# The third q/k pair of the last two heads by seven block products, and rotated rows copied back by GpSimd

## The chip, the cores and the metric

The kernel runs on one core of a Trainium2 chip. The metric is the device time of one execution in microseconds (us); three executions of the kernel before took 808.54, 808.99 and 809.23 us, so its median is 808.99 us. Five engines work beside each other: TensorE (PE) multiplies matrices, VectorE (DVE) and ScalarE (ACT) work on elements, GpSimd (POOL) does a few small operations and issues some of the DMAs, SyncE (SP) issues the other DMAs. PE writes to PSUM, the others read PSUM or SBUF; GpSimd works on SBUF alone.

## The reference, cut to what matters

One layer of an encoder trunk on 512 positions of width 1024, all in float32. The normed input `n` is projected by one large weight; of that projection, 12 heads (3 groups of dilation 1, 4 and 16, with 4 heads each) get a query and a key of 128 features per position. The first 32 features of each are rotated by position, then come windowed scores, softmax, the sum over values, and a mixture of the three groups:

```
proj = jnp.einsum('bsd,de->bse', n, w_in[l])
z_gmlp, q, k, v, gates = jnp.split(proj, split_points, axis=-1)
q = partial_rope(q.reshape(B, S, n_heads, HEAD_DIM))
k = partial_rope(k.reshape(B, S, n_heads, HEAD_DIM))
...
o_g, lse_g = dilated_window_attention(q[:, :, sl], k[:, :, sl], v[:, :, sl], dilation, window // (2 * dilation))
```

`partial_rope` gives `x1 * cos - x2 * sin` and `x2 * cos + x1 * sin` in the 32 rotated features and leaves the other 96 as they are. A gated gMLP branch, a merge, an output projection and an MLP with 4096 hidden features follow.

## The kernel before, in words

**Products of float32 by three.** Every large product splits its two operands into a high and a low part (type fp32r): ACT copies the high part (lines 74 and 79), DVE subtracts it from the value to get the low part (lines 75 and 80). PE then multiplies high by high, high by low and low by high (`mm3`, lines 84 to 86, or line 343).

**Two ways to project a q/k pair.** A pair is the query and the key of one head index in one group; its weight is a tile `qkw` of 128 x 8 x 2 x 128 (512 KB for q, 512 KB for k, loaded by SP at line 66). The plain way (`feature_tile`) takes, for q and then for k, 8 blocks of the contraction by three matmuls of 512 columns: 48 matmuls of 512 columns for a pair, into one PSUM bank each, and ACT copies the result out at line 449, once for the 32 rotated rows (`st`) and once for all 128. The other way (`seven_qk`) cuts contraction, features and positions in halves and makes the 2 x 2 block product with seven products in place of eight. Its left operands are sums of weight blocks: `seven` (lines 329 to 334) makes the sums on DVE and splits them. Each of the seven products is 4 blocks by three matmuls of 256 columns, so a pair takes 84 matmuls of 256 columns, on three of the four PSUM banks named `acc`. Between the products ACT and DVE take intermediate results out (`p1`, `z5`, `u2`, `u3`, lines 399 to 414), and a later product into the same bank waits for them. The right operands `nmov` are made once, for all positions.

**The order.** `project_qk(h)` goes through the groups of head h. Groups 0 and 1 go the seven-product way; then come the rotation of both pairs (`rotate` over 4 tiles) and the scores of group 0 (`scores_a`). Then `attend(h - 1)`, the value sums of the head before, and the loads of the values for head h (`load_v`, two DMAs on GpSimd's queue at line 305). Group 2 goes the plain way, then its rotation (2 tiles) and `scores_b`. `rotate` gathers the 32 rows of each tile in `st`, shuffles and multiplies them on DVE (lines 419 to 422), and then copies 32 x 512 back to each tile, on ACT (line 424): 6 copies for a head, 24 in all. In `scores_a` the tiles are first split by ACT and DVE (`q0h`, `q0l`, `k0h`, `k0l`).

The framework's scheduler puts each engine's instructions into a fixed order when the kernel is built: each instruction may move up as soon as its inputs are there in the scheduler's own model of time, and program order decides between several. On the chip each engine then takes its instructions in that order. Buffers come from pools with a fixed number of slots; weights and the sums `s` share three slots of the tag `raw`. The stage with the heads lies at 81 to about 245 us of the profiled execution; the gMLP part, the gates and the MLP follow.

Of the kernel before, what the change touches and what calls it, by code (L numbers as in the profile page):

```python
# [12 lines left out]
AF = mybir.ActivationFunctionType  # L13
# [23 lines left out]
def block_kernel(ctx: ExitStack, tc: tile.TileContext, x, norm_mix_pre, w_in, b_gate, ln_v_gain, ln_v_bias,  # L37
                 w_spatial, b_spatial, w_branch_a, w_branch_b, w_out, norm_mix_post, norm_mlp_pre, w_up,
                 w_down, norm_mlp_post, ident_c, rope_c, mask_c, perm_c, out):
    nc = tc.nc  # L40
# [22 lines left out]
    def wload(shape, srcs, name):  # L63
        raw = wpool.tile([P] + shape, F32, name=name, tag="raw")
        for dst, src in srcs(raw):
            nc.sync.dma_start(dst, src)
        return raw

    def wsplit(raw, pl=None, bufs=None, tag="w", sub=None):
        pl = pl or wpool  # L70
        shape = list(raw.shape)
        hi = pl.tile(shape, F32R, name="hi", tag=tag + "hi", bufs=bufs)
        lo = pl.tile(shape, F32R, name="lo", tag=tag + "lo", bufs=bufs)
        nc.scalar.activation(hi, raw, AF.Copy)  # L74
        (sub or nc.vector).tensor_tensor(lo, raw, hi.bitcast(F32), op=ALU.subtract)  # L75
        return hi, lo
# [210 lines left out]
    def feature_tile(wh, wl, nk, mh, ml, tag="acc"):  # L287
        ps = psA.tile([P, S], F32, name="pf", tag=tag, bufs={"acc": 4, "S": 2, "T": 1, "y": 1}[tag])
        for k in range(nk):
            mm3(ps, (wh[:, k], wl[:, k]), (mh[:, k], ml[:, k]), k == 0, k == nk - 1)  # L290
        return ps

    def fcols(wap, c0, nk, n, raw=None):
        return wap[:, c0:c0 + n].rearrange("(k p) c -> p k c", p=P)
# [6 lines left out]
    def load_v(h):  # L301
        hs = slice(h * HD, (h + 1) * HD)
        v0, v12 = vpool.tile([P, 2, 4, HD], F32R, name="v0s"), vpool.tile([P, 2, 4, HD], F32, name="v12s")
        for src, dst in ((v0d, v0), (v12d, v12)):
            nc.gpsimd.dma_start(dst.rearrange("p a b c -> p (a b) c"), src[:, :, :, hs].rearrange("p a b c -> p (a b) c"))
        heads[h] = v0, v12
# [77 lines left out]
    def seven_qk(raw, g, c2, c1):  # L384

        w = seven(raw.rearrange("p k r c -> p k (r c)"), wsum, wsplit, split1)
        Y, Z, X = [psA.tile([P, 512], F32, name="pg", tag="acc", bufs=4)[:, A] for _ in range(3)]
        if g:
            view = lambda ps: ps.rearrange("p (l r) -> p r l", r=4)
            half = lambda d, i: d.rearrange("p (r h l) -> p h r l", r=4, h=2)[:, i]  # L390
            snap = lambda nm: qkpool.tile([P, 4, 64], F32, name=nm)
        else:
            view = lambda ps: ps
            half = lambda d, i: d[:, (A, B)[i]]
            snap = lambda nm: qkpool.tile([P, 4, 64], F32, name=nm).rearrange("p r l -> p (r l)")
        p1, z5, u2, u3 = snap("p1"), snap("z5"), snap("u2"), snap("u3")
        product(6, Y, w, nmov, True)
        product(1, X, w, nmov, True)
        taken = nc.scalar.activation(p1, view(X), AF.Copy)
        if pending:  # L400
            with tc.issue_after(taken.ins):
                pending.pop()()
        nc.vector.tensor_tensor(u2, view(Y), p1, op=ALU.add)
        product(5, Z, w, nmov, True)
        nc.scalar.activation(z5, view(Z), AF.Copy)
        product(2, X, w, nmov, False)
        nc.scalar.activation(half(c1, 0), view(X), AF.Copy)
        product(7, Y, w, nmov, False)
        nc.vector.scalar_tensor_tensor(u3, view(Y), -1.0, p1, op0=ALU.mult, op1=ALU.subtract)
        product(3, Z, w, nmov, False)  # L410
        nc.vector.tensor_tensor(half(c1, 1), view(Z), u2, op=ALU.add)
        nc.vector.tensor_tensor(half(c2, 1), u3, z5, op=ALU.subtract)
        product(4, Y, w, nmov, False)
        nc.vector.scalar_tensor_tensor(half(c2, 0), view(Y), -1.0, p1, op0=ALU.mult, op1=ALU.subtract)

    def rotate(st, tiles, r0):
        rows = slice(r0, r0 + 32 * len(tiles))
        sw = apool.tile([P, S], F32, name="sw")
        nc.vector.stream_shuffle(sw[rows], st[rows], [(i + 16) % 32 for i in range(32)])
        nc.vector.tensor_tensor(st[rows], st[rows], rope[rows, 0], op=ALU.mult)  # L420
        nc.vector.tensor_tensor(sw[rows], sw[rows], rope[rows, 1], op=ALU.mult)
        nc.vector.tensor_tensor(st[rows], st[rows], sw[rows], op=ALU.add)
        for i, d in enumerate(tiles):
            nc.scalar.activation(d[0:32], st[r0 + 32 * i:r0 + 32 * i + 32], AF.Copy)

    def project_qk(h):
        got, tiles, r0 = {}, [], 0
        load_v(h) if not h else None
        st = apool.tile([P, S], F32, name="st", bufs=2)
        for g in range(3):  # L430
            if g == 2:
                st, tiles, r0 = apool.tile([P, S], F32, name="st", bufs=2), [], 64
                if h:
                    attend(h - 1)
                    load_v(h)
            hd0 = (g * NH + h) * HD
            raw = wload([KD, 2, P], lambda r: [(r[:, :, 0], fcols(w_in, COL_Q + hd0, KD, P)), (r[:, :, 1], fcols(w_in, COL_K + hd0, KD, P))], "qkw")
            pair = [apool.tile([P, S], F32, name=f"{nm}{g}") for nm in "qk"]
            if g < 2:
                seven_qk(raw, g, *pair)  # L440
            for j, d in enumerate(pair):
                i = r0 + 32 * len(tiles)
                if g < 2:
                    nc.scalar.activation(st[i:i + 32], d[0:32], AF.Copy)
                else:
                    ps = feature_tile(*wsplit(raw[:, :, j]), KD, nhn, nln)
                    view = ps.rearrange("p (l r) -> p r l", r=4)
                    for dst, src in ((st[i:i + 32], view[0:32]), (d, view)):
                        nc.scalar.activation(dst.rearrange("p (r l) -> p r l", r=4), src, AF.Copy)
                tiles.append(d)  # L450
                got["qk"[j], g] = d.rearrange("p (r l) -> p r l", r=4)
            if g:
                rotate(st, tiles, r0)
            if g == 1:
                scores_a(h, split_qk(tiles[:2]))
        scores_b(h, got)

    def split_qk(tiles):
        got = {}
        for nm, t in zip("qk", tiles):  # L460
            w = S if nm == "q" else S + P
            o = 0 if nm == "q" else ROT
            hi = apool.tile([P, w], F32R, name=f"{nm}0h")
            lo = apool.tile([P, w], F32R, name=f"{nm}0l")
            split_into(hi[:, o:o + S], lo[:, o:o + S], t)
            if nm == "k":
                for z, y in ((hi, nc.scalar), (lo, nc.vector)):
                    zf = z.bitcast(F32)
                    for dst, src in ((z[:, 0:ROT], zf[:, S:S + ROT]), (z[:, S + ROT:], zf[:, ROT:2 * ROT])):
                        if y is nc.scalar:  # L470
                            y.activation(dst, src, AF.Copy)
                        else:
                            y.tensor_copy(dst, src)
            got[nm, 0] = (hi, lo)
        return got
# [26 lines left out]
    def scores_a(h, got):  # L502
        md = small.tile([P, 2, 4], F32, name="mda", bufs=2)
        stat[h, "md", "a"], stat[h, "m", "a"], stat[h, "d", "a"] = md, md[:, 0], md[:, 1]
        (qh, ql), (kh, kl) = got["q", 0], got["k", 0]
        for c2 in range(2):
            ps = psA.tile([P, 2, 2, P], F32, name="psa", tag="S", bufs=2)
            for cc in range(2):
                c = 2 * c2 + cc
                qs, ks = slice(c * P, (c + 1) * P), slice(c * P, c * P + 2 * P)  # L510
                mm3(ps[:, cc], (qh[:, qs], ql[:, qs]), (kh[:, ks], kl[:, ks]), True, True)
            for cc in range(2):
                c = 2 * c2 + cc
                m = (masks[:, 0:3:2], masks[:, 1:3], masks[:, 1:3], masks[:, 1:4:2])[c]
                softmax_tile(h, "a", c, ps[:, cc], m)
# [47 lines left out]
    def attend(h):  # L563
        for _ in attend_steps(h):
            pass
# [60 lines left out]
    for h in range(NH):  # L626
        project_qk(h)
        mix(h)
# [56 lines left out]
    for g2 in range(2):  # L685
        raw = wload([KD, 2 * P], lambda r: [(r, fcols(w_in, COL_U + g2 * 2 * P, KD, 2 * P))], "uw")
        for j in range(2):
            g = 2 * g2 + j
# [405 lines left out]
```

## Time and profile before

| | |
|---|---|
| median of three executions | 808.99 us |
| the profiled execution | 808.57 us |
| its span, first to last instruction | 806.8 us |
| mean granted clock of TensorE | 0.999 |
| q/k pairs by seven products | 8 of 12 |
| copies of rotated rows on ACT | 24 |

The profile comes from one execution. Times in its rows are us from the start of its span, unless a row says ns. A row that ends with an arrow names what the engine waited for before the instruction. The rows of one engine can overlap by some hundredths of a us, since an instruction starts while the one before drains; a matmul's row is longer than the distance to the next one for the same reason, so distances between starts tell the rate.

### The profile page before, as it was taken

The numbers are of one execution on the slowest core, as the hardware profiler recorded it, in microseconds if no ns is written. First come the engines' busy times: TensorE is split into PE (matmuls) and PEld (weight loads), VectorE is DVE, ScalarE is ACT, GpSimd is POOL, SyncE is SP. The second block draws the span as 40 slices with busy tenths as digits, with TensorE's granted clock in tenths as the row PEclk, the third lists the DMA queues.
The fourth block names the chain that finished last, engine by engine and source line by source line (L and its number), as shares of the span: only waits on it lengthen the run. The fifth ranks groups of instructions, "written<-read, shape, count | busy, mean of one in ns | idle before, by whom it ended". The sixth has DMA issues, their size and how long they took to land.

```text
span 806.8 us, 12338 instructions
## 1 busy us (share of the span) xinstructions
PE 795.0 (99%) x4917; PEld 720.1 (89%) x4917; DVE 539.5 (67%) x916; ACT 423.2 (52%) x721; POOL 55.4 (7%) x85
## 2 busy tenths in 40 slices
PE   9999999999999999999999999999999999999996
PEld 6899999998988889999988899999999888888885
DVE  6784688978655878787656489988987533333324
ACT  6351467978576454554445457666666532332212
POOL 2300100010104300000001100000000000000000
PEclk9999999999999999999999999999999999999999
DMA  9733733353625433352446123333334633332202
GB/s 302 236 112 107 201 104 105 101 135 103 184 68 132 130 79 106 96 140 79 151 163 219 69 79 105 106 109 105 117 118 144 219 105 105 104 105 84 73 1 104
DMA packets 90603, 98.92 MB, mean 123 GB/s; under 512 B 2689, under 2 KB 74401, under 8 KB 90546
## 3 DMA queue, kind: packets, MB, share of 16 engines
q1 hardware_dynamic: 80208, 77.60, 31.5%
q0 software_dynamic: 10336, 20.54, 8.5%
q8 instruction: 38, 0.62, 0.3%
q14 instruction: 19, 0.16, 0.1%
q10 hardware_dynamic: 2, 0.00, 0.0%
HBM read 88.17 MB, written 9.96 MB: 122 GB/s over the span
## 4 chain that ended last, share of the span: by engine, by line
PE 93%; DVE 3%; ACT 2%; DMA 1%; issue 0%; DVEq 0%; POOLq 0%; POOL 0%; ACTq 0%
PE pacc L961 11%; PE pg L343 9%; PE pd L84 9%; PE pd L86 9%; PE pd L85 9%; PE pgacc L343 6%; PE pf L84 5%; PE pf L85 5%; PE pf L86 5%; PE ptp L961 4%; PE pv L84 4%; PE pv L86 4%; PE pv L85 4%; PE pgS L343 2%; PE psb L498 1%; PE py L617 1%
## 5 line engine op out<-in xcount | busy, mean ns | idle before, releaser
L85 PE MATMUL pd<-hl,hh 128*128 128x512 f32 x224 | 87.3, 390 | 0.0
L84 PE MATMUL pd<-hl,hh 128*128 128x512 f32 x224 | 86.3, 390 | 0.0
L86 PE MATMUL pd<-hl 128*128 128x512 f32 x224 | 86.1, 389 | 0.0
L80 DVE TENSOR_TENSOR hl<-hid,hh 128x512 fp32r<-128x512 f32 x28 | 19.2, 692 | 75.6 <-ACT hh L79 75.6
L961 PE MATMUL pacc<-nt,hl 128*128 128x256 f32 x504 | 67.7, 280 | 0.1
L79 ACT ACTIVATE hh<-hid 128x512 fp32r<-128x512 f32 x28 | 17.4, 630 | 89.0 <-PE pd L85 89.0
L961 PEld LDWEIGHTS pacc<-nt,hl 128*128 128x128 f32 x504 | 62.7, 188 | 0.5 <-ACT hl L79 0.3
L85 PEld LDWEIGHTS pd<-hl,hh 128*128 128x128 f32 x224 | 42.1, 188 | 8.8
L86 PEld LDWEIGHTS pd<-hl 128*128 128x128 f32 x224 | 42.1, 188 | 8.7
L84 PEld LDWEIGHTS pd<-hl,hh 128*128 128x128 f32 x224 | 42.0, 188 | 8.6
L80 DVE TENSOR_TENSOR hl<-dnw,hl 128x1024 fp32r<-128x1024 f32 x32 | 39.1, 1226 | 13.9 <-ACT hl L79 13.9
L961 PE MATMUL pacc<-n,hl 128*128 128x256 f32 x336 | 45.2, 280 | 0.4 <-ACT z L986 0.4
L79 ACT ACTIVATE hl<-s 128x1024 fp32r<-128x1024 f32 x28 | 29.6, 1059 | 29.1 <-DVE s L945 10.7
L84 PE MATMUL pf<-nh,hi 128*128 128x512 f32 x112 | 44.7, 399 | 0.0
L74 ACT ACTIVATE hi<-s 128x1024 fp32r<-128x1024 f32 x30 | 31.7, 1059 | 24.2 <-DVE s L330 10.8
L85 PE MATMUL pf<-nl,hi 128*128 128x512 f32 x112 | 43.9, 392 | 0.0
L86 PE MATMUL pf<-nh,lo 128*128 128x512 f32 x112 | 43.9, 392 | 0.0
L75 DVE TENSOR_TENSOR lo<-s,hi 128x1024 fp32r<-128x1024 f32 x30 | 36.6, 1224 | 9.7 <-ACT hi L74 9.6
L961 PEld LDWEIGHTS pacc<-n,hl 128*128 128x128 f32 x336 | 41.8, 188 | 0.6 <-ACT z L986 0.6
L79 ACT ACTIVATE hl<-dnw 128x1024 fp32r<-128x1024 f32 x32 | 33.5, 1049 | 12.4 <-PE pacc L961 7.5
L80 DVE TENSOR_TENSOR hl<-s,hl 128x1024 fp32r<-128x1024 f32 x28 | 34.2, 1221 | 6.3 <-ACT hl L79 6.0
L85 PE MATMUL pv<-lo,nh 128*128 128x512 f32 x96 | 38.2, 398 | 0.0
(360 smaller groups left out, 2227.3 us busy)
## 6 DMA issues: line engine op xcount, KB each, us to landing
upw<-in_w_up_dram SPq DMA_DIRECT2D x16, 1024.0 KB, 5.5
dnw<-in_w_down_dram SPq DMA_DIRECT2D x16, 1024.0 KB, 4.9
qkw<-in_w_in_dram SPq DMA_DIRECT2D x24, 512.0 KB, 5.3
gw<-in_w_in_dram SPq DMA_DIRECT2D x16, 512.0 KB, 5.4
slab<-in_w_in_dram SPq DMA_DIRECT2D x6, 1024.0 KB, 9.8
wow<-in_w_out_dram SPq DMA_DIRECT2D x4, 1024.0 KB, 5.0
w0raw<-in_w_in_dram SPq DMA_DIRECT2D x4, 512.0 KB, 7.5
v0d<-v POOLq DMA_DIRECT2D x4, 512.0 KB, 4.3
```

The lines of the kernel that those rows point to most:

```text
L74: nc.scalar.activation(hi, raw, AF.Copy)
L75: (sub or nc.vector).tensor_tensor(lo, raw, hi.bitcast(F32), op=ALU.subtract)
L79: nc.scalar.activation(hi, src, AF.Copy)
L80: return nc.vector.tensor_tensor(lo, src, hi.bitcast(F32), op=ALU.subtract)
L84: nc.tensor.matmul(ps, ah, bh, start=start, stop=False)
L85: nc.tensor.matmul(ps, ah, bl, start=False, stop=False)
L86: return nc.tensor.matmul(ps, al, bh, start=False, stop=stop)
L343: nc.tensor.matmul(ps, a[:, j], b[:, j], start=first and not (j or i), stop=(j == KH - 1 and i == 2), skip_group_check=True)
L498: nc.tensor.matmul(ps[:, rr, g - 1], got["q", g][:, r], got["k", g][:, r], start=True, stop=True)
L617: nc.tensor.matmul(o, v12[:, g, r], ptb[r // 2][:, r % 2, g], start=False, stop=(r == 3 and g == 1), skip_group_check=True)
L961: nc.tensor.matmul(ps, a[:, j], b[:, j], start=first and not (j or m), stop=(j == KH - 1 and m == 2), skip_group_check=True)
```

## The change

Two edits. The condition under which a pair goes the seven-product way is widened from groups 0 and 1 to these and group 2 of heads 2 and 3; so 10 of 12 pairs go that way, and the plain way stays for group 2 of heads 0 and 1. And in `rotate`, for all heads and groups, the copy back of the 32 rotated rows is a `tensor_copy` on GpSimd in place of an ACT copy.

```
-            nc.scalar.activation(d[0:32], st[r0 + 32 * i:r0 + 32 * i + 32], AF.Copy)
+            nc.gpsimd.tensor_copy(d[0:32], st[r0 + 32 * i:r0 + 32 * i + 32])
...
-            if g < 2:
+            block = g < 2 or h >= 2
+            if block:
                 seven_qk(raw, g, *pair)
             for j, d in enumerate(pair):
                 i = r0 + 32 * len(tiles)
-                if g < 2:
+                if block:
                     nc.scalar.activation(st[i:i + 32], d[0:32], AF.Copy)
                 else:
                     ps = feature_tile(*wsplit(raw[:, :, j]), KD, nhn, nln)
```

For the two pairs `seven_qk` runs with its group other than 0, so that it writes the rows in the order of residues (the `view` and `half` that group 1 uses).

## Rows read from the trace of the kernel before

**Rows 1.** The page: span, busy time of each engine (share of the span) and number of instructions.
```profile
span 806.8 us, 12338 instructions
PE 795.0 (99%) x4917; PEld 720.1 (89%) x4917; DVE 539.5 (67%) x916; ACT 423.2 (52%) x721; POOL 55.4 (7%) x85
```

**Rows 2.** The waits of PE from 80 to 275 us: who waited for whom, us in total, times, the longest.
```profile
PE pg L343 <- ACT p L399: 1.3, 1, 1.3
PE pt L593 <- DVE ptal L80: 0.4, 1, 0.4
PE py L617 <- ACT ptb L595: 0.2, 1, 0.2
```

**Rows 3.** Busy time of each engine in three stretches of the stage with the heads: length, then PE, weight loads, DVE, ACT and POOL, each with its instructions, granted clock, share of the DMA engines, GB/s.
```profile
115.00:155.00 40.00, 40.00 (x297) 38.02 (x296) 36.49 (x92) 33.28 (x70) 0.00 (x0) 1.00 0.35 92
155.00:192.00 37.00, 37.00 (x274) 35.05 (x273) 30.76 (x81) 27.88 (x61) 2.34 (x3) 1.00 0.48 129
192.00:228.00 36.00, 34.71 (x250) 32.43 (x249) 22.70 (x69) 27.20 (x59) 2.34 (x3) 1.00 0.45 132
```

**Rows 4.** The chain of waits, in order of time: start, us, engine, tile and line.
```profile
177.45 1.42 PE pg L343 x12
...
187.27 0.60 ACT k L449
...
188.81 0.51 ACT q L424
189.35 0.63 ACT k L424
...
191.75 0.63 ACT q L424
192.39 0.64 ACT k L424
...
193.67 0.28 ACT p L399
...
198.64 1.43 PE pg L343 x12
```

**Rows 5.** Timeline of PE, the first and the last of 18 matmuls of 512 columns in a row, of the plain pair of head 2: start, us.
```profile
178.72 0.39 PE L84 MATMUL pf<-nh,hi 128*128 128x512 f32 x1
...
182.58 0.39 PE L86 MATMUL pf<-nh,lo 128*128 128x512 f32 x1
```

**Rows 6.** The instructions on the tile `qkw`: duration in ns as shortest/median/longest, first and last start, form. Eight pairs go the seven-product way (lines 329 to 334 and `ar`, `a`), four the plain way (lines 74 and 75, twice each).
```profile
L80 DVE TENSOR_TENSOR ar<-qkw,ar x16: 680/689/694, 55.7 to 202.3; 128x512 fp32r<-128x512 f32 x16
L329 DVE TENSOR_TENSOR s<-qkw x8: 1205/1224/1226, 57.2 to 181.6; 128x1024 f32<-128x1024 f32 x8
L330 DVE TENSOR_TENSOR s<-s,qkw x8: 673/688/692, 60.1 to 185.1; 128x512 f32<-128x512 f32 x8
L75 DVE TENSOR_TENSOR lo<-qkw,hi x8: 1215/1224/1226, 92.7 to 208.4; 128x1024 fp32r<-128x1024 f32 x8
```

**Rows 7.** A group of DVE instructions from 80 to 240 us, one of the five of 256 columns that a seven-product pair needs to take its results out: us busy, mean ns, idle time before.
```profile
L412 DVE TENSOR_TENSOR q<-u,z 128x256 f32<-128x256 f32 x8 | 3.4, 422 | 0.2
```

**Rows 8.** Groups of ACT instructions from 80 to 240 us: us busy, mean ns, idle time before.
```profile
L424 ACT ACTIVATE k<-st 32x512 f32<-32x512 f32 x12 | 7.6, 630 | 0.2
L424 ACT ACTIVATE q<-st 32x512 f32<-32x512 f32 x12 | 7.5, 626 | 3.9 <-DVE st L422 3.7
L449 ACT ACTIVATE st<-pf 32x512 f32<-32x512 f32 x8 | 4.7, 587 | 3.6 <-PE pf L86 3.5
L79 ACT ACTIVATE ar<-qkw 128x512 fp32r<-128x512 f32 x14 | 8.8, 629 | 2.8 <-PE pg L343 2.3 <-DMA qkw<-in_w_in_dram 0.4
```

**Rows 9.** Timeline of DVE: start, us, instruction; first two neighbours, then one instruction with GpSimd idle and the same beside a GpSimd operation, then one that reads PSUM.
```profile
182.68 0.68 DVE L420 TENSOR_TENSOR st<-st,rope 128x512 f32<-128x512 f32 x1
183.29 0.68 DVE L421 TENSOR_TENSOR sw<-sw,rope 128x512 f32<-128x512 f32 x1
...
176.99 0.16 DVE L536 TENSOR_TENSOR z<-e,mab 128x4 f32<-128x4 f32 x1
...
250.28 2.36 DVE L536 TENSOR_TENSOR z<-e,mab 128x4 f32<-128x4 f32 x1 [0.83 <-ACT e L534]
...
257.78 1.29 DVE L648 SCALAR_TENSOR_TENSOR gt<-gt,pv 128x512 f32<-128x512 f32 x2 [0.22 <-ACT gt L647]
```

**Rows 10.** Timeline of POOL (start, us, and the idle time before with its releaser).
```profile
165.44 0.88 POOL L305 DMA_DIRECT2D v0s<-v0d  x1 [75.65 <-PE pg L343]
...
250.23 2.39 POOL L75 TENSOR_TENSOR lo<-uw,hi 128x1024 fp32r<-128x1024 f32 x1 [6.28 <-ACT hi L74]
252.57 0.93 POOL L305 DMA_DIRECT2D v0s<-v0d  x1
256.87 2.38 POOL L75 TENSOR_TENSOR lo<-uw,hi 128x1024 fp32r<-128x1024 f32 x1 [3.37 <-ACT hi L74]
```

**Rows 11.** Groups of POOL instructions by shape over the whole span: us busy, mean ns.
```profile
L200 POOL TENSOR_TENSOR w0lo<-w0raw,w0hi 128x512 fp32r<-128x512 f32 x2 | 2.6, 1292 | 0.3 <-ACT w0hi L199 0.3
L101 POOL MEMSET sedge<- 128x56 f32 x1 | 0.1, 145 | 0.0
```

**Rows 12.** Timeline of SP: start of the loads of the gMLP weight that follow the heads' weights.
```profile
197.22 6.13 SPq L66 DMA_DIRECT2D slab<-in_w_in_dram  x2
```

**Rows 13.** Timeline of ACT: the first split of that weight.
```profile
214.27 1.06 ACT L74 ACTIVATE hi<-slab 128x1024 fp32r<-128x1024 f32 x1 [1.60 <-PE pg L343]
```

## Prediction

> **What bounds the kernel now.** I read the page first. PE is busy for 99% of the span and everything else far less, DVE 67% and ACT 52% [rows 1], so a change pays by the PE time it removes or by a wait of PE that it ends. Next, the waits of PE in the stage that the edits touch: from 80 to 275 us there are three, 1.9 us together, and 1.3 of them is one [rows 2]. Then the engines by stretch, cut about where one head follows another: PE has nearly no gap, but DVE is at 36.49 of 40 us around head 1, 30.76 of 37 around head 2, and 22.70 of 36 around head 3 [rows 3]. The average of 67% hides that DVE is nearly full just there. Last, the chain through the one long wait: PE waits for `p` (line 399), because ACT works off a row of copies before it [rows 4].
>
> The sum is made on the profiled execution: span 806.8 us and 1.77 us around it make 808.57 us, which is 0.42 us under the median of the runs shown. I add that 0.42 at the end.
>
> **The change part by part.**
>
> *PE.* A plain pair is 48 matmuls of 512 columns. From the first to the last of 18 in a row are 3.86 us for 17 distances [rows 5], 0.227 us each, so 10.9 us for a pair. A seven-product pair is 7 products of 12 matmuls; a product took 1.42 and 1.43 us on the chain [rows 4], so 10.0 us. Each pair exchanged takes 0.9 us from PE, two take 1.8 us. All of it lies on the path, as PE does nothing else there. This is the only sure gain, and it is small: 0.22% of the time.
>
> *DVE, two pairs.* A seven-product pair needs three sums (1.22 + 0.69 + 0.69; the second and third are alike), two low parts of 1024 (1.22 each) and three of 512 (0.69 each) [rows 6], and five short operations on the banks at 0.42 [rows 7]: 9.2 us by durations, against 2.4 us for the two low parts of a plain pair, which go. But neighbours overlap: instructions of 0.68 us start 0.61 us apart [rows 9]; less 0.08 for each of the eight instructions by which a pair grows (ten for two), the 6.8 us are 6.2 us of busy time. Around head 3 they are covered: 22.7 + 6.2 = 28.9 of 36 us. Around head 2 they aren't quite: 30.8 + 6.2 = 37.0 us in a stretch that PE would now finish in 36.1. What is late next are the operations between the products.
>
> *ACT.* The two pairs lose 4 copies of about 0.59 each at line 449 and gain three high parts of 0.63 and two copies into `st` of about the same [rows 8] and three copies out of the banks of 0.28 [rows 4]: +1.6 us a pair. All heads together lose 24 copies of 0.63, 15.1 us [rows 8]. ACT has 4 to 9 us free in each stretch [rows 3], so the sum itself is worth nothing; what counts is the one wait. Before `p` at 193.67 ACT ran without a gap, and four of the pieces on that chain, 2.4 us, are copies of line 424, and one more comes from line 449 [rows 4]. Both kinds are gone there. I take the 1.3 us wait as ended. Bounds: 0, if another wait takes its place, to 1.9, if all three go.
>
> *The copies on GpSimd.* No such copy is in the trace. Below, a memset of 128x56 took 0.145 us; above, a subtraction with two inputs of 512 took 1.29 [rows 11]. I take 0.65, half of the latter, as a copy has one input. GpSimd's time is no matter (24 x 0.65 = 16 us, where 55 of 807 are busy [rows 1]); two other things are.
>
> First, its queue. What is queued behind a copy that waits for `st` are the loads of the next head's values (line 305), the store of the finished head, and later the low parts of the gMLP weight (line 75). The loads themselves wait long: one stood idle for 75.65 us until 165.44 [rows 10]. A copy behind that one would be late by tens of us. But the queue is not in program order: the subtraction at 250.23 belongs to a later part of the program than the load that follows it at 252.57 [rows 10], so each goes in when the scheduler thinks it is ready, and the copies should come ahead of the load. I take nothing for this.
>
> Second, what it does to DVE. The instruction of line 536 takes 0.16 us; beside a GpSimd subtraction that began at 250.23 and took 2.39, it took 2.36 and ended with it. Line 648, which reads PSUM and one SBUF tile, ran at its usual 0.65 each beside the subtraction of 256.87 [rows 9, 10]. So a DVE operation with two SBUF inputs stands still while GpSimd reads SBUF, and the low parts, the sums and the rotations are of that kind. The Trainium skill ("SBUF — State Buffer", section "Who interferes with whom") states this as a rule: the shared pair of ports is an exclusive lock, taken by whoever starts first for the whole instruction; the trace agrees (2.36 in place of 0.16), though whether a copy with one input holds DVE as a subtraction does no row shows. By that rule each copy can cost DVE its whole length, and the copy in turn waits out a DVE operation.
>
> The bound for this is nothing (GpSimd waits, DVE doesn't) to 1.29 us a copy. I take the mean hold as 0.2 us a copy: about a third of the copies meet such an operation after they start, and on average half of the 0.65 us or a bit more is left. Some 14 of the copies fall into 115 to 192 us (two heads and the start of a third), so 2.8 us there. Idle DVE time in that stretch is 77 - 67.25 = 9.75 us [rows 3]; less the 6.2 of head 2 that leaves 3.5. It fits, narrowly. PE pays only where a late DVE operation stands between two products: I take 1.0 us for that, from 0 (around head 1 DVE is at 91% and PE waited for nothing over 0.4 us [rows 2, 3]) to the rival's price below.
>
> "GPSIMD Engine Reference" of the Trainium skill, section "Performance versus the Vector engine", gives 1.8 cycles an element at 1.2 GHz for its best loop; by that a copy would be 0.77 us (an estimate), and the hold would rise by a fifth. The sum would still fit.
>
> *Loads.* Each of the two pairs takes a second slot of three for its sums, so later weights load later by one slot. The first load of the gMLP weight starts at 197.22 [rows 12] and its first split at 214.27 [rows 13], 17 us later. One pair's step of about 10 us is covered; nothing is taken.
>
> *Sum.* -1.8 (products) - 1.3 (the wait of ACT) + 1.0 (late DVE operations) = -2.1 us: 806.5 us against 808.57, 806.9 us on the median. Its own range: 805.3 to 808.2, from the bounds of the wait and of the late operations.
>
> **The rivals.**
>
> *DVE is held and becomes the bound* (slower). Place: 115 to 192 us. It decides from a mean hold of 3.5 / 14 = 0.25 us a copy, just above what I took. At 0.65, a copy's whole length each time, the 14 copies cost 9.1 us, 5.6 over what is idle: 808.57 - 1.8 - 1.3 + 5.6 + 0.42 = 811.5 us; at 1.29 it would be 820 (18.1 us, 14.6 over). For it speaks that the scheduler's order can't be relied on to leave room for a hold, and that most of DVE's time there goes to operations with two SBUF inputs. Against it: DVE stood idle behind ACT's copies before, and what comes late there can slip into the stretch of head 3, where DVE would still have 7 us free (36 - 28.9).
>
> *The gain is eaten.* The plain pair needs two splits and then runs 10.9 us of PE work that waits for nothing; it was what PE could turn to while DVE caught up between products. Without it, new waits of 1 us for each of the two pairs and a further 1 us for late copies cancel the 3.1: about 808.6 to 809, no change.
>
> *Only the good happens.* No new wait, and the other two waits vanish: 808.57 - 1.8 - 1.9 + 0.42 = 805.3, and a little less where the scores come sooner: 805.
>
> **How the numbers follow.** Forecast 0.53, DVE held 0.25, gain eaten 0.14, only the good 0.08. About 0.2% (1.6 us) is what a measurement of this kernel can tell from no change, so faster means under 807.4. Of the forecast's range four fifths lie under that: 0.42 + 0.08 = 0.50 for faster. The same: the last fifth, most of the eaten gain and a little of the held DVE, 0.11 + 0.12 + 0.03 = 0.26. Slower: 0.24. The range of 804.9 to 811.0 leaves out the worse half of the held DVE (0.12) and some of the best case.
>
> **What would show it.** In the profile after: 840 matmuls at line 343 from `qkw` pairs in place of 672, 0.9 us less of PE for each exchanged pair; no wait of PE for `p` of line 399 over a few tenths; POOL with 24 copies of about 0.65 us; DVE near full around head 2. It would be wrong if DVE instructions of 0.6 us stretch to 1.2 beside the copies and PE shows waits for DVE of several us between 115 and 192; or if the copies start long after their `st`, behind a load.

## The result and the profile after

The changed kernel took 810.72 us (median of 19 runs, 809.19 to 812.12), the kernel before 808.73 us on the same chips (19 runs, 807.83 to 809.67). The ratio is 1.0027, interval 1.0021 to 1.0033: slower by 2 us where 2.1 us less were forecast. The profiled execution took 810.98 us, with a span of 809.2 us against 806.8 [rows 1].

The page after, span and busy time (columns as in [rows 1]):

```profile
span 809.2 us, 12541 instructions
PE 794.1 (98%) x4989; PEld 722.3 (89%) x4989; DVE 555.4 (69%) x938; ACT 412.3 (51%) x705; POOL 77.0 (10%) x109
```

72 more matmuls are two exchanged pairs (84 for 48 each). PE worked 0.9 us less and stood still more: 15.1 us of the span against 11.8 (806.8 - 795.0). DVE is busy 15.9 us more, where two pairs were to bring 12.4 and the holds of all 24 copies 4.8. The waits of PE from 80 to 275 us of the changed kernel, against [rows 2]:

```profile
PE py L618 <- ACT ptb L596: 1.2, 1, 1.2
PE pg L343 <- DVE nm L487: 1.2, 1, 1.2
PE pg L343 <- DVE xd L550: 1.0, 1, 1.0
PE pg L343 <- DVE u L409: 0.8, 2, 0.6
PE psa L85 <- DVE k0l L474: 0.3, 1, 0.3
PE pg L343 <- DVE q L414: 0.3, 1, 0.3
PE pt L594 <- DVE rs_in L90: 0.3, 1, 0.3
PE pt L581 <- DVE nm L487: 0.2, 1, 0.2
```

The one long wait of before, ACT's `p`, is gone, as forecast. In its place stand mainly waits for DVE before a product (`pg` L343), and one for ACT. (Behind line 438 the changed kernel's numbers are higher by one.) The same stretches as [rows 3], in the changed kernel:

```profile
115.00:155.00 40.00, 39.50 (x287) 37.11 (x287) 37.15 (x90) 29.14 (x63) 9.34 (x10) 1.00 0.33 89
155.00:192.00 37.00, 34.88 (x294) 34.29 (x293) 32.68 (x84) 23.27 (x53) 8.48 (x9) 1.00 0.39 100
192.00:228.00 36.00, 34.82 (x289) 34.09 (x288) 31.82 (x86) 24.23 (x56) 4.64 (x6) 1.00 0.50 147
```

Read the third number after the stretch's length: DVE still has 2.9, 4.3 and 4.2 us idle. PE lacks 2.1 us in the second stretch, where it had no gap before. So DVE wasn't full (32.7 of 37 us around head 2, where 37.0 were forecast), and PE waited for it all the same. The copies and the DVE groups beside them, in the groups from 80 to 245 us (us busy, mean ns, idle before):

```profile
L424 POOL COPY k<-st 32x512 f32<-32x512 f32 x12 | 11.9, 990 | 0.7
L424 POOL COPY q<-st 32x512 f32<-32x512 f32 x12 | 9.6, 798 | 93.3 <-DVE st L422 81.3 <-DVE cf L542 11.7
...
L412 DVE TENSOR_TENSOR q<-u,z 128x256 f32<-128x256 f32 x10 | 5.0, 501 | 0.2
L420 DVE TENSOR_TENSOR st<-st,rope 64x512 f32<-64x512 f32 x4 | 3.4, 844 | 0.1
```

A copy takes 0.80 or 0.99 us on the mean where ACT took 0.63 [rows 8], and line 412 grew from 422 ns [rows 7] to 501. How that happens shows in two timelines of the changed kernel, POOL first (start, us):

```profile
187.42 1.08 POOL L424 COPY q<-st 32x512 f32<-32x512 f32 x1 [6.94 <-DVE cf L542]
188.56 1.50 POOL L424 COPY k<-st 32x512 f32<-32x512 f32 x1
190.11 0.61 POOL L424 COPY q<-st 32x512 f32<-32x512 f32 x1
190.78 0.96 POOL L424 COPY k<-st 32x512 f32<-32x512 f32 x1
```

and DVE, with the idle time before an instruction in brackets:

```profile
174.34 1.23 DVE L329 TENSOR_TENSOR s<-qkw 128x1024 f32<-128x1024 f32 x1 [3.97 <-DMA qkw<-in_w_in_dram]
175.48 0.14 DVE L487 TENSOR_SCALAR nm<-mdb 128x1 f32<-128x1 f32 x1
...
177.44 0.42 DVE L409 SCALAR_TENSOR_TENSOR u<-pg,p 128x256 f32<-128x256 f32 x1
177.77 0.20 DVE L487 TENSOR_SCALAR nm<-mdb 128x1 f32<-128x1 f32 x2
...
188.29 1.30 DVE L329 TENSOR_TENSOR s<-qkw 128x1024 f32<-128x1024 f32 x1 [0.25 <-DMA qkw<-in_w_in_dram]
...
190.34 0.93 DVE L330 TENSOR_TENSOR s<-s,qkw 128x512 f32<-128x512 f32 x1
191.19 0.83 DVE L412 TENSOR_TENSOR q<-u,z 128x256 f32<-128x256 f32 x1
```

The copy of 188.56 started while the sum of 188.29 ran and took 1.50 us: it ended 0.47 us after the sum, which ended at 189.59, so it stood for most of the sum. The copy of 190.11 ran alone in 0.61; the DVE instruction of 190.34, which takes 0.69 elsewhere [rows 6], met it and took 0.93, and the next copy made line 412 take 0.83. So each holds the other.

The first lines show the other thing: DVE's queue stood 3.97 us at the sum of the next pair, because its weight had not landed, with `u3` (line 409, at 177.44) some way behind it. PE paid 1.2 us of it, in the timeline of PE:

```profile
177.91 0.39 PE L343 MATMUL pg<-nt,ar 128*128 128x256 f32 x1 [1.20 <-DVE nm L487]
...
194.31 0.35 PE L343 MATMUL pg<-nt,hi 128*128 128x256 f32 x1 [1.01 <-DVE xd L550]
```

The releaser that this view names (`nm` at 177.77) is only the DVE instruction that ended last; the product needs the `u3` just before it, which reads the bank.

That weight is asked for late. SP issues the load of head 3's first pair here, in the changed kernel (start, us):

```profile
166.01 0.99 SPq L66 DMA_DIRECT2D qkw<-in_w_in_dram  x2
```

and in the kernel before here:

```profile
156.82 1.00 SPq L66 DMA_DIRECT2D qkw<-in_w_in_dram  x2
```

### The profile page after: what moved, and what is told of

Its sections match the earlier page's. It is cut to its first block, busy times and chain, and to the rows that moved or that the text cites. A ratio compares the mean times of both kernels' runs of the same rounds, so it can differ in the third digit from the quotient of the medians.

```text
span 809.2 us, 12541 instructions
## 1 busy us (share of the span) xinstructions
PE 794.1 (98%) x4989; PEld 722.3 (89%) x4989; DVE 555.4 (69%) x938; ACT 412.3 (51%) x705; POOL 77.0 (10%) x109
## 4 chain that ended last, share of the span: by engine, by line
PE 86%; DVE 7%; ACT 2%; DMA 2%; issue 1%; DVEq 0%; POOLq 0%; POOL 0%; SPq 0%; ACTq 0%
PE pacc L962 11%; PE pd L85 9%; PE pd L86 9%; PE pd L84 9%; PE pg L343 7%; PE pgacc L343 6%; PE ptp L962 5%; PE pf L84 4%; PE pf L85 4%; PE pf L86 4%; PE pv L85 3%; PE pv L86 3%; PE pv L84 3%; PE pgS L343 2%; DMA qkw<-in_w_in_dram 2%
## 5 line engine op out<-in xcount | busy, mean ns | idle before, releaser
L74 ACT ACTIVATE hi<-s 128x1024 fp32r<-128x1024 f32 x34 | 35.9, 1058 | 26.2 <-DVE s L330 12.8
L75 DVE TENSOR_TENSOR lo<-s,hi 128x1024 fp32r<-128x1024 f32 x34 | 41.6, 1226 | 8.9 <-ACT hi L74 8.8
L343 PE MATMUL pg<-nt,hi 128*128 128x256 f32 x240 | 44.8, 282 | 1.3 <-DVE xd L550 1.0
L343 PEld LDWEIGHTS pg<-nt,hi 128*128 128x128 f32 x240 | 37.1, 188 | 1.9 <-ACT z L405 1.2
L86 PE MATMUL pv<-hi,nl 128*128 128x512 f32 x96 | 37.6, 397 | 0.0
```

Source lines behind the costliest of these rows:

```text
L86: return nc.tensor.matmul(ps, al, bh, start=False, stop=stop)
L343: nc.tensor.matmul(ps, a[:, j], b[:, j], start=first and not (j or i), stop=(j == KH - 1 and i == 2), skip_group_check=True)
```

## The experiments

Two theories to begin with. *Hold*: the copies on GpSimd hold DVE, and the price is the same in whatever order the instructions stand. *Order*: the two edits together give the scheduler another order of all engines, in which a weight is late and DVE's queue blocks. The runs of before beside each kernel gave 808.18 to 808.84 us.

**One edit at a time.** The first edit alone (the copies stay on ACT):

```
-            nc.gpsimd.tensor_copy(d[0:32], ...)
+            nc.scalar.activation(d[0:32], ..., AF.Copy)
```

> Only the first edit: group 2 of heads 2 and 3 by seven products, the rotated rows still copied by ACT. Theory DVE load (the 12 us that the two pairs add to DVE, which has no room around heads 2 and 3, make the new PE gaps): slower than before by 1.5 to 3 us, with several PE waits for DVE between 170 and 210 us. Theory copies (GpSimd's slower, mutually blocking copies make them): faster by about 1.8 us, PE gaps near the 1.9 us of before. If both are needed: within 1 us of before.

Measured 806.39 us, ratio 0.9976 (0.9967 to 0.9985). The second edit alone:

```
-            block = g < 2 or h >= 2
+            block = g < 2
```

> Only the second edit: rotated rows copied by GpSimd, all third pairs the plain way. Theory DVE load: within 1 us of before, perhaps 1 us faster as the ACT wait of 1.3 us goes. Theory copies: slower by 1.5 to 4 us, with PE waits for DVE soon after the copies. If both are needed: within 1 us of before.

Measured 809.22 us, 1.0010 (1.0001 to 1.0019). Then the first edit for one pair only, with the copies on ACT and on GpSimd:

```
-            block = g < 2 or h >= 2
+            block = g < 2 or h == 3
```

> Seven products for group 2 of head 3 alone, copies on ACT. Theory DVE load: around head 3 DVE has 13 us free and 6 are added, so no new gap: faster than before by 0.5 to 1.5 us. Theory copies: the gain of one pair, 0.9 us faster. If the scheduler's new order as such decides, anything within 2 us either way.

> Seven products for group 2 of head 3 alone, copies on GpSimd. Theory DVE load: faster than before by 1 to 2 us (0.9 for the pair, and the ACT wait of 1.3 us gone). Theory copies: slower than the same kernel with copies on ACT by 1.5 to 4 us, so slower than before by 1 to 3 us.

Measured 809.11 us, 1.0006 (0.9997 to 1.0015), and 807.38 us, 0.9984 (0.9975 to 0.9993). What follows: the first edit gains about what its own steps say; the second alone costs 0.4 us by the medians and 0.8 by the ratio (interval 0.1 to 1.5); and together they cost 4 us more than the first alone. With one pair the sign of the second edit turns round. No sum of fixed prices gives these numbers.

**The hold alone.** To hold DVE with nothing else changed, ACT makes the real copies and GpSimd copies the same rows a second time into a tile that nobody reads. In the traces the order of PE, DVE and ACT is then, instruction by instruction, that of the kernel without these copies, and no engine waits for one of them. The first edit alone was timed again beside it:

> The first edit alone once more, for its profile. Theory order (each combination of the two edits gets its own fixed order from the scheduler, and that of both edits together is a bad one): 806.4 us again, PE gaps between 80 and 275 us of about 1 to 2 us, and the load of head 3's first weight lands before DVE needs it. If that load is late by 4 us here as well, the load isn't what costs the changed kernel its time.

```
-            nc.gpsimd.tensor_copy(d[0:32], st[...])
+            nc.scalar.activation(d[0:32], st[...], AF.Copy)
+            nc.gpsimd.tensor_copy(spare[0:32], st[...])
```

> The first edit alone, the rotated rows still copied by ACT, and beside each ACT copy the same rows copied by GpSimd to a spare tile that nobody reads: PE, DVE, ACT and SP have the very order of the first edit alone, and only GpSimd's 24 copies are added. Theory hold (a copy on GpSimd holds DVE's operations with two SBUF inputs): slower than the first edit alone by 2 to 4 us, about 809 to 810. Theory order: the hold alone costs under 1 us, so 806.4 to 807.4.

The same 24 copies beside the kernel before (on the same chip), and the changed kernel again, on another chip, that of the next two kernels:

> The kernel before, with the same 24 copies on GpSimd to a spare tile beside ACT's copies; the order on PE, DVE, ACT and SP is that of before. Theory hold: slower than before by 1 to 3 us (DVE is less loaded here than with the two exchanged pairs). Theory order: within 0.8 us of before.

> The changed kernel itself, beside the next two on one chip. 0.2 to 0.35% slower than before; DVE waits 4 us for head 3's first weight at about 170 us.

Measured, in this order: 806.60 us, 0.9979 (0.9970 to 0.9988); 808.0, 0.9997 (0.9988 to 1.0006); 809.53, 1.0016 (1.0008 to 1.0025); 810.58, 1.0026 (1.0017 to 1.0035). The hold costs 1.4 us in the one order and 1.3 in the other, each pair of kernels on one chip. The changed kernel is 4.0 us over the first edit alone by the medians and 3.8 by the ratios, across two chips; so about 2.5 us are something else. The waits of PE from 80 to 275 us with the first edit alone:

```profile
PE pt L581 <- ACT p L558: 0.5, 1, 0.5
PE pt L594 <- DVE ptal L80: 0.4, 1, 0.4
PE py L618 <- ACT ptb L596: 0.2, 1, 0.2
```

Its stretches, as in [rows 3]:

```profile
155.00:192.00 37.00, 36.43 (x306) 35.64 (x305) 34.50 (x91) 31.39 (x70) 2.34 (x3) 1.00 0.40 100
192.00:228.00 36.00, 36.00 (x290) 35.13 (x290) 29.52 (x81) 27.14 (x59) 2.34 (x3) 1.00 0.63 191
```

DVE is busier here than in the changed kernel around head 2 (34.50 of 37), and no product waits for it. With the copies beside it, the waits of PE are these:

```profile
PE pg L343 <- DVE u L409: 0.7, 1, 0.7
PE pt L594 <- DVE ptal L80: 0.4, 1, 0.4
PE psa L85 <- DVE k0l L474: 0.4, 1, 0.4
PE pg L343 <- DVE lo L75: 0.3, 1, 0.3
PE pt L581 <- ACT p L558: 0.3, 1, 0.3
PE py L618 <- ACT ptb L596: 0.2, 1, 0.2
```

Comparing the means of the DVE groups (80 to 245 us) of the same form, the copies beside add 2.9 us over all of them, 0.12 us a copy. In the changed kernel it is 4.9 us, of which 1.8 are one instruction of line 522 beside a GpSimd subtraction at 244.38; the other 3.0 are 0.13 us a copy, if all of it is put down to the copies.

**The late weight.** Four kernels go at it in the changed kernel. In the first the load of head 1's values that lands beside the weight is cut from 512 to 64 KB, into head 0's tile, so that head 1's output isn't computed from its own values (the order of PE, DVE and ACT stays):

```
-            nc.gpsimd.dma_start(dst..., src...)
+            m = 1 if h == 1 and dst is v0 else 8
+            nc.gpsimd.dma_start(dst...[:, :m], src...[:, :m])
```

> The changed kernel with one DMA made light: of head 1's group 0 values only an eighth is loaded (64 KB in place of 512; the rest stays what head 0 left), so head 1's output in group 0 isn't computed from its own values. PE, DVE, ACT and SP keep the changed kernel's very order, and that DMA is the one that runs beside the load of head 3's first weight. Theory late load (DVE stands 4 us behind that load, with the softmax of head 1 queued behind it, and the PE gaps from 176 to 194 us, 3.1 us, follow from it): the load lands about 2 to 3 us sooner, the wait of DVE falls to 1 to 2 us, and the kernel is 1 to 2 us faster than the changed one. If DVE's load or the copies' holds alone make the gaps: less than 0.5 us faster.

Measured 810.46 us, 1.0030 (1.0018 to 1.0041). DVE's wait fell from 3.97 to 2.61 us, and PE's gap of 1.20 us at 177.91 is gone: with the order unchanged, that gap is shown to come from the late weight. But the next wait for a weight rose from 0.25 to 1.75, and PE's wait for `u3` behind it from 0.65 to 2.05, so nothing was gained. In this kernel's PE timeline:

```profile
189.94 1.70 PE L343 MATMUL pg<-nt,ar 128*128 128x256 f32 x12 [2.05 <-DVE u L409]
```

In the second the last split of head 2's second weight, which frees the slot that the load waits for, goes before the first split of the next weight (as it does with the first edit alone, where the load starts at 161.93):

```
+        with tc.issue_after(<the split ar1 of head 2, group 1>):
             <the split ar0 of head 2, group 2>
```

> The changed kernel with one more rule for the scheduler: the first split of group 2 of head 2 comes after the last split of group 1 (the one that frees the slot into which head 3's first weight is loaded), on ACT and DVE, as in the order of the first edit alone. Theory late load: the load is issued some us sooner, DVE waits for it under 1.5 us, and the kernel is 1.5 to 2.5 us faster than the changed one, near the 808.0 us of the first edit with copies beside. If the order of these two splits doesn't matter: within 0.7 us of the changed kernel.

Measured 808.66 us, 1.0002 (0.9993 to 1.0011): 1.9 us better than the changed kernel, but not as meant. The load starts at 165.81, nearly as late as there (166.01). It lands sooner: 5.6 us after its issue, where it took 7.8. Here the load of values on GpSimd's queue was issued at 166.56, behind both DMAs of the weight, and there at 166.17, between them; that this is the reason isn't shown. The sum waits 1.12 us for the weight, and PE's gap at 177.91 is gone. So is most of its wait for `ptb`, 0.17 us in place of 1.20, though all 24 copies are on GpSimd here too; its wait for `u3` behind the next weight is 1.39 us. The one rule also moved many other instructions, so this isn't a test of the late weight alone. In the third, in head 3, the sum that blocks the queue is issued only behind `u3` of the pair before:

```
+        with tc.issue_after(<u3 of the pair before>):
             nc.vector.tensor_tensor(s[:, :, 0:4:2], ...)
```

> The changed kernel with a rule for the scheduler: in head 3 the first sum of a pair (line 329, which waits for the pair's weight) comes on DVE behind the subtraction u3 (line 409) of the pair before. Theory blocked queue (DVE takes its instructions in a fixed order, the sum stands in front of short operations that PE needs, and while its weight isn't there these wait too): the PE waits for u of line 409 and for nm, 2 us of the 5.3, go, and the kernel is 1 to 2 us faster than the changed one. If DVE is simply full there: within 0.7 us of the changed kernel.

Measured 818.89 us, 1.0138 (1.0123 to 1.0154): the cure is far worse. PE now waits 1.67 and 1.68 us for `hi` (line 74), the split of a sum that comes late for its own pair, 2.10 us for `ptah`, and 2.95 us for `p` (line 558) behind the last head. Last, the sums get a buffer of their own, so that weights have three slots (room taken from two other pools):

```
-        w = seven(raw..., wsum, wsplit, split1)
+        w = seven(raw..., lambda: qkpool.tile([P, KH, 4, P], F32, name="sq"), wsplit, split1)
...
-    ppool = pool(attn, "ppool", bufs=15)
+    ppool = pool(attn, "ppool", bufs=12)
...
-            t = ppool.tile([P, 2, 2, P], F32, name="ptb", bufs=2)
+            t = ppool.tile([P, 2, 2, P], F32, name="ptb", bufs=1)
```

> The changed kernel, but in the heads' stage the sums have a slot of their own and the three raw slots hold weights alone; for the room the softmax tiles p have 12 slots in place of 15 and the turned tiles ptb one in place of two. Theory late load: head 3's weights are there long before DVE needs them, no DVE wait for qkw over 0.3 us, and the kernel is 1.5 to 3 us faster than the changed one, unless the smaller pools make new waits. If the copies' holds and their way through GpSimd make the gaps: within 1 us of the changed kernel.

Measured 812.21 us, 1.0044 (1.0031 to 1.0057). No sum waits for a weight any more, and around head 2 it shows, but not around head 1. The stretches of this kernel:

```profile
155.00:192.00 37.00, 36.10 (x308) 35.88 (x307) 35.55 (x88) 25.16 (x59) 9.30 (x10) 1.00 0.38 100
...
115.00:155.00 40.00, 37.67 (x276) 35.48 (x275) 35.07 (x87) 27.44 (x60) 8.29 (x10) 1.00 0.33 87
```

PE's gap in the first is 0.90 us against 2.12 in the changed kernel. All three waits that make up the 2.12 are gone, those of 177.91 (1.20), 182.01 (0.28) and 189.97 (0.65); the 0.90 is another one, before the scores:

```profile
161.84 0.39 PE L85 MATMUL psa<-k0l,q0h 128*128 128x256 f32 x1 [0.90 <-DVE k0l L80]
```

In the second stretch the gap is 2.33 us against 0.50, and behind the heads, at 271.56, PE waits 1.84 us for `vln` (line 680). For the 2.33 this kernel's DVE timeline shows:

```profile
117.30 1.00 DVE L420 TENSOR_TENSOR st<-st,rope 64x512 f32<-64x512 f32 x1
118.22 1.10 DVE L421 TENSOR_TENSOR sw<-sw,rope 64x512 f32<-64x512 f32 x1
...
122.54 1.63 DVE L329 TENSOR_TENSOR sq<-qkw 128x1024 f32<-128x1024 f32 x1
124.10 0.41 DVE L409 SCALAR_TENSOR_TENSOR u<-pg,p 128x256 f32<-128x256 f32 x1
```

Three instructions stretched by 0.3, 0.4 and 0.4 us stand before the `u3` for which PE waits 2.3 us in this run; the rest of that wait isn't accounted for, and whether the smaller pools have a part in it wasn't tested.

**Order or copies.** Shortening the GpSimd copies, so that the last positions are not copied back, changes the scheduler's order at some lengths and hardly at others:

```
-            nc.gpsimd.tensor_copy(d[0:32], st[...])
+            nc.gpsimd.tensor_copy(d[0:32, :504], st[..., :504])
```

> The changed kernel with each GpSimd copy cut from 512 to 504 columns (the last 8 positions of the rotated rows are not copied back); the order of VectorE and ScalarE is that of the changed kernel but for one exchange of neighbours. Both theories: as the changed kernel, 810.2 to 810.7 us, ratio 1.0026. It is the control for the next.

> Copies of 480 columns (the last 32 positions are not copied back): the copies are 5% shorter than in the run before, but the scheduler's order is another one from about the second head on. Theory (the 2.5 us belong to the order, in which the next pair's weight is asked for late and VectorE's queue waits for it): the order decides, so the time leaves 810.4 by 1 us or more, most likely down, to 807.5 to 809. Rival (the copies themselves): 5% less copying is worth 0.2 us at most, 810.2.

> Copies of 448 columns (the last 64 positions are not copied back), in the order of the 480 run but for two or three neighbours. Theory: within 0.4 us of the 480 run. Rival: the copies' length counts, another 0.3 us off on top of what 480 gave, on the way to 808 at half the length.

> Copies of 256 columns (the second half of the positions is not copied back), in a third order. Theory: the hold halves, 0.7 us less than at 512, and the order adds its own one or two us up or down: 807 to 809.5. Rival: in proportion to the length, 4.2 / 2 = 2.1 us less than the changed kernel, 808.4, and the 480 and 448 runs lie on the straight line between.

Measured: 810.13 us, 1.0020 (1.0011 to 1.0029); 810.48, 1.0021 (1.0012 to 1.0030); 811.24, 1.0030 (1.0018 to 1.0042); 808.17, 1.0001 (0.9991 to 1.0010). The other order of 480 columns didn't move the time, against my theory; half the length gave 2 us, as the rival had it, but in a third order, so that both can claim it; 448 columns came out 0.8 us above 480, where the theory allowed 0.4 and the rival a fall; the intervals overlap, so this decides nothing. Last, the copies of one rotation alone on GpSimd, of group 2 and then of groups 0 and 1:

```
+            if len(tiles) == 2:    # 4 in the second kernel
                 nc.gpsimd.tensor_copy(d[0:32], ...)
+            else:
+                nc.scalar.activation(d[0:32], ..., AF.Copy)
```

> First edit whole; of the copies back only the 8 of group 2 (the rotation over 2 tiles) are on GpSimd, the 16 of groups 0 and 1 on ScalarE. Theory (the place is the rotation of groups 0 and 1, where four copies in a row stand before the splits and scores_a): little is lost here, the hold of 8 copies, 0.5 us: 806.5 to 807.3. Rival (each copy costs the same, 4 us / 24 = 0.17 us, wherever it stands): 1.3 us over the first edit alone, 807.8. A new order may add or take a us in either case.

> First edit whole; the 16 copies of groups 0 and 1 on GpSimd, the 8 of group 2 on ScalarE. Theory: nearly all of the loss is here, 809.8 to 810.6. Rival (each copy the same): 16 x 0.17 = 2.7 us over the first edit alone, 809.2. Had the loss its place at group 2, it would be 807.

Measured 811.48 us, 1.0034 (1.0021 to 1.0046), and 817.64 us, 1.0116 (1.0102 to 1.0129). Both theories of these two runs fall: 8 copies on GpSimd cost no less than 24 (the intervals overlap), and 16 cost 11 us over none, of which 3 us are one wait of PE for `p` behind the last head and 3.4 us a fallen clock (last section). Neither the number of the copies nor their place sets the price.

What does follow the time is PE's idle time from 80 to 275 us (195 less the busy time of that stretch), in all kernels with ten pairs by seven products. It is read from the one profiled execution, whose time stands beside it and can differ from the median, by 3.3 us in the kernel with GpSimd for group 2. "Clock" is one less the granted clock, added up over stretches of 1 us from 80 to 280 us, the most that PE can have lost by it:

| kernel | PE idle, us | clock, us | profiled execution, us | median, us |
|---|---|---|---|---|
| copies on ACT | 1.2 | 0 | 805.93 | 806.60 |
| and 24 more beside on GpSimd | 2.3 | 0 | 807.93 | 808.0 |
| 256 columns | 3.3 | 0 | 807.68 | 808.17 |
| split first | 3.7 | 0 | 809.01 | 808.66 |
| 480 columns | 4.8 | 1.7 | 811.83 | 810.48 |
| 448 columns | 5.1 | 0 | 810.70 | 811.24 |
| changed kernel | 5.3 | 0 | 810.98 | 810.72 |
| light values | 5.3 | 0 | 809.92 | 810.46 |
| 504 columns | 5.5 | 0 | 810.13 | 810.13 |
| own buffer for the sums | 6.1 | 0 | 810.24 | 812.21 |
| GpSimd for group 2 | 6.8 | 1.7 | 814.78 | 811.48 |
| GpSimd for groups 0 and 1 | 7.8 | 3.4 | 817.73 | 817.64 |
| sums late | 9.7 | 3.4 | 817.88 | 818.89 |

The profiled execution's time less the two columns is 804.1 to 806.5 us in every row. This tells where the time goes, in this stage and through PE, and not yet why.

## Why the prediction was wrong

**Products.** Right. With the first edit alone PE's busy time over the span is 2.3 us lower (792.7 against 795.0), 1.8 us of it forecast, and the time fell by 1.6 to 2.5 us. In the changed kernel PE's busy time is only 0.9 us lower; these runs don't account for the difference.

**The wait of ACT.** The wait for `p` of line 399 is gone in the changed kernel as well as with the first edit alone, which keeps the copies on ACT. It is gone with the second edit alone, too. So either edit ends it, and the second wasn't needed, against the step that counted the copies of line 424 in. It was worth less than 1.3 us net: with the first edit alone PE's idle time in the stage falls from 1.9 to 1.2 us, as another wait, for `p` of line 558 (0.5 us), came; with the second edit alone waits of 1.7 us for line 680 came. (ACT's free time in the three stretches was 6.7 to 9.1 us [rows 3], not 4 to 9; nothing hangs on it.)

**DVE, two pairs.** Right in what it meant, a quarter too high in size: the first edit adds 10.0 us of DVE time (549.5 against 539.5), 12.4 forecast; around head 2 DVE is busy for 34.5 us, 37.0 forecast, and no product waits for it.

**The copies on GpSimd.** The length was 0.60 us alone, 0.65 taken. By "GPSIMD Engine Reference" of the Trainium skill, section "Performance versus the Vector engine", it would have been 0.77, an estimate; the measurement decides. The copies came ahead of the loads in POOL's queue, as taken. The hold is 0.12 to 0.13 us of DVE time a copy, 0.2 taken; 16 copies fell into 115 to 192 us, 14 taken. The rule of the Trainium skill ("SBUF — State Buffer", section "Who interferes with whom"), an exclusive lock for whoever starts first, holds for a copy with one input too: 0.61 to 1.50 us for the copy, 0.69 to 0.93 for DVE.

**Where it failed: "It fits, narrowly", and "I take 1.0 us for that".** That step set the holds against the idle DVE time of a stretch and let PE pay 1.0 us. The hold measured by itself cost 1.3 to 1.4 us, near enough. But the changed kernel pays 4.0 us over the first edit alone, with 11.4 us of DVE time idle in the three stretches, and the sign that the prediction named came, if small: PE waits 2.6 us for DVE between 115 and 192. The idle time of an engine that takes its queue in order isn't a store: it lies where the queue waits for something else, and an instruction that PE needs stands behind. The rival "DVE is held and becomes the bound" forecast 811.5 us, close to the result, but from a mean hold of 0.65 us and a DVE out of idle time; neither came.

**Where it failed: "Loads ... nothing is taken".** Only the gMLP weight was looked at. The next pair's weight moved from 156.82 to 166.01, because its slot is freed later, and DVE's queue stood 3.97 us. With the first edit alone it had moved to 161.93, and DVE didn't wait for it; the rest came with the order of both edits. PE paid 1.2 us at 177.91. That gap went when the load beside the weight was made light, and with a buffer of their own for the sums; neither kernel was faster, as other waits came.

**What no step had.** Each edit makes the scheduler write a new order for all engines, and that alone moved the time by 1.9 us (a rule for one split) to 8 us (sums late, 3.4 of it the clock), and differently for each set of copies. Part of it lies behind the last head, in waits that no step priced: PE waits there 1.20 us for `ptb` in the changed kernel, 0.17 with the first edit alone, 1.84 for `vln` with the sums' own buffer, and 2.95 for `p` with the sums late. I took an order to stay as it was and priced edits on it.

**What stays open.** Of the 4.0 us, 1.4 are shown as the hold, in the order of the first edit alone. The rest is read off the trace, against the first edit with copies beside: 1.2 us are the gap of the late weight, and 1.0 the longer wait for `ptb`. The latter goes with the order and not with the copies as such, since it is 0.17 us in the split-first and about 0.2 in the 480-column kernel, which have all 24 copies on GpSimd. What is left lies mainly in the waits of 194.31 and 182.01; the wait of 189.97 isn't part of it, as the kernel with copies beside has one like it (0.69). Whether the copies' own lateness has a share, these runs don't settle: no kernel had the order of the first edit alone and real copies on GpSimd, as every edit that put them there changed the order. So the way from the second edit to the whole of the 4.0 us isn't shown.

**Which is best.** The first edit alone, 0.9976 and 0.9979 of the time before in two series, beats both kernels.

## What to carry to other kernels

Price a small edit in a scheduled kernel by its parts, each timed alone: the two here gave about -2 and +0.6 us alone and +2 together, and moving a light copy off an engine that was no longer waited for cost more than the other edit had won. Idle time of an in-order engine doesn't pay for delays; look which instruction that the bound engine needs stands behind the delayed one. And when an edit takes more slots of a shared pool, follow the very next load through that pool, not only the last.

## What the runs showed of the hardware

A gap of PE can cost more than its length. In the profiled execution of the kernel with GpSimd for group 2 (814.78 us, 3.3 over that kernel's median) a late weight again blocked DVE, here for 6.21 us (its DVE timeline):

```profile
175.74 1.23 DVE L329 TENSOR_TENSOR s<-qkw 128x1024 f32<-128x1024 f32 x1 [6.21 <-DMA qkw<-in_w_in_dram]
```

PE then waited 2.38 us (its PE timeline):

```profile
178.66 2.02 PE L343 MATMUL pg<-nt,ar 128*128 128x256 f32 x12 [2.38 <-DVE u L409]
```

and these are its stretches of 1 us around it (the third number from the right is the granted clock):

```profile
177.00:178.00 1.00, 0.00 (x0) 0.00 (x0) 1.00 (x2) 0.00 (x0) 0.00 (x0) 1.00 0.09 29
178.00:179.00 1.00, 0.34 (x3) 0.34 (x3) 1.00 (x4) 0.73 (x1) 0.00 (x0) 1.00 0.02 8
179.00:180.00 1.00, 1.00 (x10) 1.00 (x9) 1.00 (x4) 0.33 (x1) 0.49 (x1) 0.91 0.00 0
180.00:181.00 1.00, 1.00 (x7) 1.00 (x6) 1.00 (x4) 0.32 (x1) 0.08 (x1) 0.50 0.43 156
...
183.00:184.00 1.00, 1.00 (x10) 1.00 (x9) 1.00 (x3) 0.95 (x3) 0.00 (x0) 0.88 0.00 0
184.00:185.00 1.00, 1.00 (x10) 1.00 (x10) 1.00 (x6) 1.00 (x2) 0.00 (x0) 1.00 0.20 45
```

PE is at work again from 178.66, and about 1 us later the clock falls to 0.50, the 1.2 GHz level, and stays there until about 183.2. Over 179 to 184 us the clock lacks 0.09 + 3 x 0.50 + 0.12 = 1.7 us, on top of the 2.4 of the gap. The gaps of 1.2 and 1.0 us in the changed kernel's profile left the clock at 1.00. But a gap needn't be longer than these: with 480 columns PE stood 0.44 us before 193.35 and 1.13 us before 194.98, and the clock was 0.64, 0.50, 0.50 and 0.65 in the four stretches of 1 us from 195 on, another 1.7 us. In the two slowest kernels PE stood 2.95 and 2.96 us for `p` of the softmax near 270 us, and the clock lacks 3.4 us in each; from 228 to 275 us it is 0.95 (sums late) and 0.96 on the mean. That is part of why the time climbs so fast at the foot of the table.
